# Attention scores on one core: half of the first casts on ScalarE, the first transposes copied by both engines, and an even spread of transposing steps

## The chip, the cores and the metric

The kernel runs on one core of a Trainium2 chip. The metric is the device time of one execution in microseconds (us), the median of several runs. A profile's span is about 1.8 us shorter than the timed run it belongs to (200.7 against 202.5), because it starts and ends with recorded instructions. Some executions are slower, at a lower granted TensorE clock; they are called slow here (in one kernel below 170.88 us at a clock of 0.77, where its fast ones took 164.4 to 166.6 at 0.93 to 0.97).

Engine names in the profile: PE is TensorE's matmuls, PEld its weight loads, DVE is VectorE, ACT is ScalarE, POOL is GpSimd, SP is SyncE, whose queue issues the transfers. HBM is the chip's main memory, SBUF the core's working memory, and PSUM the memory into which the matmuls write. The DMA engines move the bytes of a transfer, in packets; the DMA queue is the list of transfers that they are given. To evacuate is to copy a result out of PSUM.

## The reference

For q and k of shape (8, 8, 512, 64) in float32 the kernel computes all scaled products:

```python
scale = 1.0 / np.sqrt(q.shape[-1])
return (np.einsum('bhqd,bhkd->bhqk', q, k) * scale).astype(np.float32)
```

The inputs are 16.78 MB and the output is 67.11 MB. Nothing can be left out of either, so 83.89 MB have to pass between HBM and SBUF.

## The kernel before

The work is cut into four units (two batches each) and each unit into four store tiles of 4.19 MB. A unit's keys and queries are loaded (2.10 MB each), cast to bfloat16, transposed on PE through PSUM (tile `tp`), and copied into `kT` and `qz`. Score matmuls then fill PSUM tiles `ps`, and ACT and DVE in turn scale them into an SBUF tile `big`, which is stored. Load tiles and store tiles share the three buffers of `big`.

```python
big_pool = ctx.enter_context(tc.tile_pool(name="big", bufs=3))
tpsum_pool = ctx.enter_context(tc.tile_pool(name="tpsum", bufs=2, space=bass.MemoryType.PSUM))
psum_pool = ctx.enter_context(tc.tile_pool(name="psum", bufs=2, space=bass.MemoryType.PSUM))
# ... (cut)
def load_and_cast(v):
    xf = big_pool.tile([P, 2, 2, J * D], f32, name="big")
    both = []
    for x, src in enumerate((k_r, q_r)):
        nc.sync.dma_start(out=xf[:, x], in_=src[v].rearrange("p (s c) -> p s c", s=2))
    for x in range(2):
        xb = bf_pool.tile([P, JP, 2, D, 2], bf16, name="xb")
        wide = (1, RO)[x]
        for s in range(2):
            pinned(nc.gpsimd.tensor_copy(
                out=xb[:, :, s].rearrange("p (g i) d e -> p g e i d", i=wide),
                in_=xf[:, x, s].rearrange("p (g e i d) -> p g e i d", e=2, i=wide, d=D)))
        # ... (cut)

def rearrange(tp, pattern, dst):
    nonlocal n_tp
    copy = (nc.vector.tensor_copy, nc.scalar.copy)[n_tp % 2]
    n_tp += 1
    for s in range(2):
        src = tp[half(s)].rearrange(pattern, n=N, h=2)
        for h in range(2):
            pinned(copy(out=dst(s, h), in_=src[:, h]))
            yield
# ... (cut)
cast = [load_and_cast(v) for v in range(UNITS)]
ts = {}
for _ in transpose(0, *cast[0]):
    pass
for v in range(UNITS):
    ahead = transpose(v + 1, *cast[v + 1]) if v + 1 < UNITS else iter(())
    for t in range(TILES):
        for n, _ in enumerate(scores(v, t)):
            take(ahead, 1 if v == 0 else int(n in (0, 2, 3, 5, 6)))
```

`transpose` is a generator of 20 steps (four transpose tiles, each one step of matmuls and four copies). `take` weaves these steps of the next unit between the eight evacuations of a store tile. The casts write every second bfloat16 element, so that a pair of sequence positions forms one 4-byte word for the transposes.

Of the kernel before, what the change touches and what calls it, by code (L numbers as in the profile page):

```python
# [1 line left out]

# [5 lines left out]


@with_exitstack  # L10
def kernel(
    ctx: ExitStack,
    tc: tile.TileContext,
    q: bass.AP,
    k: bass.AP,
    out: bass.AP,
):







    nc = tc.nc
    B, H, S, D = q.shape
    scale = 1.0 / (D ** 0.5)
    P = 128
    UNITS = B // 2
    N = H  # L30
    M = P // (2 * H)
    R = S // M
    J = R // 2
    RO = 8
    U = S // RO
    JP = J // 2
    JJ = J // RO // 2
    W = 8
    IW = W // JJ
    TILES = N // 2  # L40

    f32 = mybir.dt.float32
    bf16 = mybir.dt.bfloat16

    q_r = q.rearrange("(v b) g (m j) d -> v (b g m) (j d)", b=2, j=R)
    k_r = k.rearrange("(v b) g (m j) d -> v (b g m) (j d)", b=2, j=R)
    out_r = out.rearrange("(v b) (t x h) (u i) k -> v (b t) (h u) x (i k)", b=2, x=2, h=2, i=RO)

    consts = ctx.enter_context(tc.tile_pool(name="consts", bufs=1))

    big_pool = ctx.enter_context(tc.tile_pool(name="big", bufs=3))
    bf_pool = ctx.enter_context(tc.tile_pool(name="bf", bufs=6))
    t_pool = ctx.enter_context(tc.tile_pool(name="t", bufs=2))
    tpsum_pool = ctx.enter_context(tc.tile_pool(name="tpsum", bufs=2, space=bass.MemoryType.PSUM))
    psum_pool = ctx.enter_context(tc.tile_pool(name="psum", bufs=2, space=bass.MemoryType.PSUM))


    pinned = tc.keep_in_program_order

    n_evac = 0  # L60
    n_tp = 0

    def evacuate(dst, src):
        nonlocal n_evac
        if n_evac % 2 == 0:
            pinned(nc.scalar.mul(out=dst, in_=src, mul=scale))  # L66
        else:
            pinned(nc.vector.tensor_scalar(out=dst, in0=src, scalar1=scale, scalar2=None,  # L68
                                           op0=mybir.AluOpType.mult))
        n_evac += 1  # L70

    def half(h):
        return slice(h * D, (h + 1) * D)

    def words(ap):
        return ap.bitcast(f32)

    def load_and_cast(v):

        xf = big_pool.tile([P, 2, 2, J * D], f32, name="big")  # L80
        both = []
        for x, src in enumerate((k_r, q_r)):
            nc.sync.dma_start(out=xf[:, x], in_=src[v].rearrange("p (s c) -> p s c", s=2))
        for x in range(2):
            xb = bf_pool.tile([P, JP, 2, D, 2], bf16, name="xb")

            wide = (1, RO)[x]
            for s in range(2):
                pinned(nc.gpsimd.tensor_copy(  # L89
                    out=xb[:, :, s].rearrange("p (g i) d e -> p g e i d", i=wide),  # L90
                    in_=xf[:, x, s].rearrange("p (g e i d) -> p g e i d", e=2, i=wide, d=D)))
            both.append(words(xb.rearrange("p j s d e -> p j (s d e)")))
        return both

    def rearrange(tp, pattern, dst):

        nonlocal n_tp
        copy = (nc.vector.tensor_copy, nc.scalar.copy)[n_tp % 2]
        n_tp += 1
        for s in range(2):  # L100
            src = tp[half(s)].rearrange(pattern, n=N, h=2)
            for h in range(2):
                pinned(copy(out=dst(s, h), in_=src[:, h]))  # L103
                yield

    def transpose(v, kb, qb):


        kT = t_pool.tile([P, N, M, 2, J], bf16, name="kT")
        qz = qzs[v % 2]  # L110
        ts[v] = (kT, qz)
        kw = words(kT)
        qw = words(qz)
        for j0 in range(0, JP, W):
            tp = tpsum_pool.tile([P, W, P], f32, name="tp")
            for j in range(W):
                pinned(nc.tensor.transpose(out=tp[:, j, :], identity=identity, in_=kb[:, j0 + j]))  # L117
            yield
            yield from rearrange(tp, "d j (n h m) -> d h n m j",
                                 lambda s, h: kw[half(h), :, :, s, j0:j0 + W])  # L120
        for i0 in range(0, RO, IW):
            tp = tpsum_pool.tile([P, IW, JJ, P], f32, name="tp")
            for i in range(IW):
                for jj in range(JJ):
                    pinned(nc.tensor.transpose(out=tp[:, i, jj, :], identity=identity,  # L125
                                               in_=qb[:, RO * jj + i0 + i]))
            yield
            yield from rearrange(tp, "d i jj (n h m) -> d h i n m jj",
                                 lambda s, h: qw[half(h), i0:i0 + IW, :, h * U // 2:(h + 1) * U // 2]
                                 .rearrange("d i n (m s jj) -> d s i n m jj", s=2, jj=JJ)[:, s])  # L130

    def scores(v, t):

        kT, qz = ts[v]
        o = big_pool.tile([P, 2, RO, S], f32, name="big")
        for x in range(2):
            n = 2 * t + x
            for i in range(0, RO, 2):
                ps = psum_pool.tile([P, 2, S], f32, name="ps")
                for w in range(2):  # L140
                    pinned(nc.tensor.matmul(out=ps[:, w, :], lhsT=qz[:, i + w, n, :],  # L141
                                            rhs=kT[:, n].rearrange("d m s j -> d (m s j)"),
                                            start=True, stop=True))
                evacuate(o[:, x, i:i + 2, :], ps)
                yield
        nc.sync.dma_start(out=out_r[v, t], in_=o.rearrange("p x i k -> p x (i k)"))  # L146

    def take(steps, count):
        for _ in range(count):
            next(steps, None)  # L150

    identity = consts.tile([P, P], dtype=f32)
    make_identity(nc, identity)
    qzs = [consts.tile([P, RO, N, P], bf16, name=f"qz{n}") for n in range(2)]
    for qz in qzs:
        nc.vector.memset(qz, 0.0)  # L156
    cast = [load_and_cast(v) for v in range(UNITS)]

    ts = {}
    for _ in transpose(0, *cast[0]):  # L160
        pass
    for v in range(UNITS):
        ahead = transpose(v + 1, *cast[v + 1]) if v + 1 < UNITS else iter(())
        for t in range(TILES):
            for n, _ in enumerate(scores(v, t)):

                take(ahead, 1 if v == 0 else int(n in (0, 2, 3, 5, 6)))
        for _ in ahead:
            pass


# [1 line left out]
_INS = ['q', 'k']  # L173
_OUTS = [((8, 8, 512, 512), 'float32')]


# [23 lines left out]
```

## Time and profile before

| | before |
|---|---|
| time, median of 3 | 202.47 us (202.41 to 202.62) |
| DMA packets' share of 16 engines' span | 98.3% |
| DVE, PE, ACT, POOL busy | 106.8, 105.3, 85.0, 39.5 us of 200.7 |
| first store issued | 36.81 us |

The table of groups (line, engine, operation, output<-input, shapes, count | busy us, mean ns of one | idle us before it and what ended most of it):

```profile
L89 POOL CAST xb<-big 128x2048 bf16<-128x2048 f32 x16 | 38.8, 2468 | 7.9 <-DMA big<-in_k_dram 7.3
...
L103 ACT COPY kT<-tp 64x512 f32<-64x512 f32 x16 | 9.2, 577 | 15.3 <-PE tp L117 15.1
L103 DVE COPY kT<-tp 64x512 f32<-64x512 f32 x16 | 11.0, 686 | 6.3 <-PE tp L117 6.0
```

The timeline of the first unit's copies on ACT, and then of the same on DVE (start us, us, engine, line, operation, count, idle before it):

```profile
17.15 2.35 ACT L103 COPY kT<-tp 64x512 f32<-64x512 f32 x4 [15.13 <-PE tp L117]
22.21 2.50 ACT L103 COPY qz<-tp 64x512 f32<-64x512 f32 x4 [2.70 <-PE tp L125]
```

```profile
15.45 2.79 DVE L103 COPY kT<-tp 64x512 f32<-64x512 f32 x4 [6.04 <-PE tp L117]
20.71 2.80 DVE L103 COPY qz<-tp 64x512 f32<-64x512 f32 x4 [2.47 <-PE tp L125]
```

Each engine takes a whole transpose tile, four copies in a row, and the two overlap: DVE is at its tile from 15.45 to 18.24, ACT starts on the other at 17.15.

### The profile page before, as it was taken

The numbers are of one execution on the slowest core, as the hardware profiler recorded it, in microseconds if no ns is written. First come the engines' busy times: TensorE is split into PE (matmuls) and PEld (weight loads), VectorE is DVE, ScalarE is ACT, GpSimd is POOL, SyncE is SP. The second block draws the span as 40 slices with busy tenths as digits, with TensorE's granted clock in tenths as the row PEclk, the third lists the DMA queues.
The fourth block names the chain that finished last, engine by engine and source line by source line (L and its number), as shares of the span: only waits on it lengthen the run. The fifth ranks groups of instructions, "written<-read, shape, count | busy, mean of one in ns | idle before, by whom it ended". The sixth has DMA issues, their size and how long they took to land.

```text
span 200.7 us, 1143 instructions
## 1 busy us (share of the span) xinstructions
PE 105.3 (52%) x384; PEld 45.8 (23%) x384; DVE 106.8 (53%) x98; ACT 85.0 (42%) x97; POOL 39.5 (20%) x22
## 2 busy tenths in 40 slices
PE   0035758566657465478637496748585667510000
PEld 0034535223214131224313122312121111100000
DVE  6705538486475976485749357844444444630000
ACT  2004423864755629253844384366435243620000
POOL 1299999995000000000000000000000000000000
PEclk9999576999699999957999759975858858975555
DMA  6999999999999999999999999999999999999994
GB/s 206 424 444 437 421 421 441 434 395 421 434 424 441 428 431 431 433 426 434 431 428 424 434 441 424 431 431 434 424 431 434 431 424 431 428 437 428 428 428 199
DMA packets 5509, 83.95 MB, mean 418 GB/s; under 512 B 384, under 2 KB 384, under 8 KB 384
## 3 DMA queue, kind: packets, MB, share of 16 engines
q1 hardware_dynamic: 5504, 83.89, 98.3%
q8 instruction: 3, 0.05, 0.1%
q14 instruction: 2, 0.02, 0.0%
HBM read 16.78 MB, written 67.11 MB: 418 GB/s over the span
## 4 chain that ended last, share of the span: by engine, by line
DMA 40%; DVE 10%; PE 8%; ACT 6%; issue 1%; ACTq 0%; SPq 0%; DVEq 0%
DMA out_dram<-big 40%; DVE big L68 9%; PE ps L141 8%; ACT big L66 5%; ACT qz L103 1%; DVE qz L103 1%; ACTq L66 0%; SPq L146 0%; DVEq L68 0%
## 5 line engine op out<-in xcount | busy, mean ns | idle before, releaser
L141 PE MATMUL ps<-kT,qz 128*128 128x512 bf16 x256 | 87.6, 447 | 55.5 <-ACT big L66 41.6
L68 DVE TENSOR_SCALAR big<-ps 128x1024 f32<-128x1024 f32 x64 | 78.4, 1224 | 59.8 <-PE ps L141 37.2
L66 ACT ACTIVATE big<-ps 128x1024 f32<-128x1024 f32 x64 | 65.5, 1023 | 73.0 <-PE ps L141 37.2
L141 PEld LDWEIGHTS <-qz 128*128 128x128 bf16 x256 | 27.2, 106 | 111.0 <-issue 97.5
L89 POOL CAST xb<-big 128x2048 bf16<-128x2048 f32 x16 | 38.8, 2468 | 7.9 <-DMA big<-in_k_dram 7.3
L117 PE MATMUL tp<-identity,xb 128*128 128x128 f32 x64 | 11.6, 346 | 13.4 <-POOL xb L89 13.4
L103 ACT COPY kT<-tp 64x512 f32<-64x512 f32 x16 | 9.2, 577 | 15.3 <-PE tp L117 15.1
L103 DVE COPY kT<-tp 64x512 f32<-64x512 f32 x16 | 11.0, 686 | 6.3 <-PE tp L117 6.0
L117 PEld LDWEIGHTS tp<-identity,xb 128*128 128x128 f32 x64 | 10.5, 184 | 15.2 <-POOL xb L89 13.4
L103 DVE COPY qz<-tp 64x512 f32<-64x512 f32 x16 | 11.0, 687 | 2.7 <-PE tp L125 2.5
L103 ACT COPY qz<-tp 64x512 f32<-64x512 f32 x16 | 9.6, 602 | 2.9 <-PE tp L125 2.7
L125 PE MATMUL tp<-identity,xb 128*128 128x128 f32 x64 | 9.4, 300 | 2.5 <-ACT kT L103 2.5
L125 PEld LDWEIGHTS tp<-identity,xb 128*128 128x128 f32 x64 | 8.5, 156 | 4.3 <-issue 3.3
L156 DVE MEMSET qz<- 128x4096 uint32 x2 | 6.9, 3472 | 2.5 <-PEq L184 1.7
L103 ACT ACT_TABLE_LOAD x1 | 1.3, 1283 | 0.7 <-PEq L184 0.7
masks.py:199 POOL TENSOR_SCALAR_AFFINE_SELECT identity<-identity 128x128 f32<-128x128 f32 x1 | 0.3, 292 | 0.1
masks.py:197 POOL MEMSET identity<- 128x128 f32 x1 | 0.2, 204 | 0.3 <-POOLq L184 0.3
L184 POOL MEMSET const-float32-0.0<- 128x1 f32 x1 | 0.1, 98 | 0.2 <-issue 0.2
L184 POOL MEMSET const-bfloat16-1.0<- 128x1 bf16 x1 | 0.1, 101 | 0.0
L184 POOL MEMSET const-uint8-127<- 128x1 uint8 x1 | 0.1, 101 | 0.0
L184 POOL MEMSET const-float32-1.0<- 128x1 f32 x1 | 0.1, 98 | 0.0
## 6 DMA issues: line engine op xcount, KB each, us to landing
out_dram<-big SPq DMA_DIRECT2D x16, 4096.0 KB, 20.7
big<-in_k_dram SPq DMA_DIRECT2D x4, 2048.0 KB, 18.1
big<-in_q_dram SPq DMA_DIRECT2D x4, 2048.0 KB, 22.7
```

Of the source, the lines that this page charges most:

```text
L66: pinned(nc.scalar.mul(out=dst, in_=src, mul=scale))
L68: pinned(nc.vector.tensor_scalar(out=dst, in0=src, scalar1=scale, scalar2=None, op0=mybir.AluOpType.mult))
L89: pinned(nc.gpsimd.tensor_copy(out=xb[:, :, s].rearrange("p (g i) d e -> p g e i d", i=wide), in_=xf[:, x, s].rearrange("p (g e i d) -> p ...
L103: pinned(copy(out=dst(s, h), in_=src[:, h]))
L117: pinned(nc.tensor.transpose(out=tp[:, j, :], identity=identity, in_=kb[:, j0 + j]))
L125: pinned(nc.tensor.transpose(out=tp[:, i, jj, :], identity=identity, in_=qb[:, RO * jj + i0 + i]))
L141: pinned(nc.tensor.matmul(out=ps[:, w, :], lhsT=qz[:, i + w, n, :], rhs=kT[:, n].rearrange("d m s j -> d (m s j)"), start=True, stop=True))
L156: nc.vector.memset(qz, 0.0)
L184: nc = _bacc.Bacc("TRN2", target_bir_lowering=False, num_devices=1)
```

## The change

The intent is to bring the first scores forward: while POOL casts one half of an array, ACT casts the other; both engines share each of the first transposes; and unit 1's transposing is spread over four store tiles instead of two and a half. Loads and casts are separated, so that ACT's casts of unit 1 stand after the first copies in its order.

```diff
-    def load_and_cast(v):
+    def load(v):
         xf = big_pool.tile([P, 2, 2, J * D], f32, name="big")
...
+    def cast(v, xf):
...
-                pinned(nc.gpsimd.tensor_copy(
+                to_bf16 = nc.scalar.copy if s and v < 2 else nc.gpsimd.tensor_copy
+                pinned(to_bf16(
...
-        copy = (nc.vector.tensor_copy, nc.scalar.copy)[n_tp % 2]
+        copies = (nc.vector.tensor_copy, nc.scalar.copy)
+        first = len(ts) == 1
...
-                pinned(copy(out=dst(s, h), in_=src[:, h]))
+                pinned(copies[(n_tp + h * first) % 2](out=dst(s, h), in_=src[:, h]))
...
-    cast = [load_and_cast(v) for v in range(UNITS)]
+    xfs = [load(v) for v in range(3)]
 
     ts = {}
-    for _ in transpose(0, *cast[0]):
+    for _ in transpose(0, *cast(0, xfs[0])):
         pass
+    xfs.append(load(3))
+    casts = [None] + [cast(v, xfs[v]) for v in range(1, UNITS)]
...
-                take(ahead, 1 if v == 0 else int(n in (0, 2, 3, 5, 6)))
+                take(ahead, int(n in (0, 2, 3, 5, 6)))
```

More of the change, by code (lines that the diff above doesn't have):

```diff
@@ L76, in words @@
         return ap.bitcast(f32)
-    def load_and_cast(v):
+    def load(v):
         xf = big_pool.tile([P, 2, 2, J * D], f32, name="big")
-        both = []
         for x, src in enumerate((k_r, q_r)):
             nc.sync.dma_start(out=xf[:, x], in_=src[v].rearrange("p (s c) -> p s c", s=2))
+        return xf
+    def cast(v, xf):
+        both = []
         for x in range(2):
@@ L156 @@
         nc.vector.memset(qz, 0.0)
-    cast = [load_and_cast(v) for v in range(UNITS)]
+    xfs = [load(v) for v in range(3)]
     ts = {}
-    for _ in transpose(0, *cast[0]):
+    for _ in transpose(0, *cast(0, xfs[0])):
         pass
+    xfs.append(load(3))
+    casts = [None] + [cast(v, xfs[v]) for v in range(1, UNITS)]
     for v in range(UNITS):
-        ahead = transpose(v + 1, *cast[v + 1]) if v + 1 < UNITS else iter(())
+        ahead = transpose(v + 1, *casts[v + 1]) if v + 1 < UNITS else iter(())
         for t in range(TILES):
             for n, _ in enumerate(scores(v, t)):
-                take(ahead, 1 if v == 0 else int(n in (0, 2, 3, 5, 6)))
+                take(ahead, int(n in (0, 2, 3, 5, 6)))
         for _ in ahead:
```

## The prediction

> **What bounds the kernel now.** I read the 40 slices first, then the DMA queue, the table of windows, the SyncE queue's own waits, and only then the groups of instructions. In the slices, the DMA row is the mean busy share of the 16 DMA engines and the row below it is what they moved:
>
> ```profile
> DMA  6999999999999999999999999999999999999994
> GB/s 206 424 444 437 421 421 441 434 395 421 434 424 441 428 431 431 433 426 434 431 428 424 434 441 424 431 431 434 424 431 434 431 424 431 428 437 428 428 428 199
> ...
> q1 hardware_dynamic: 5504, 83.89, 98.3%
> ```
>
> Only the first and the last slice are below 9. One queue carries all 83.89 MB (16.78 MB of loads, 67.11 MB of stores) and its packets fill 98.3% of the span of 16 engines. No compute engine is above 53%: DVE 106.8 us and PE 105.3 us of 200.7. The table of windows (columns: stretch, its length, busy us of PE, PEld, DVE, ACT, POOL with counts, clock, DMA share, GB/s) shows where the transfer rate falls short:
>
> ```profile
> 0.00:2.00 2.00, 0.00 (x0) 0.00 (x0) 0.34 (x1) 1.26 (x1) 0.70 (x6) 1.00 0.42 82
> 2.00:4.00 2.00, 0.00 (x0) 0.00 (x0) 2.00 (x1) 0.02 (x1) 0.00 (x0) 1.00 0.65 221
> ...
> 40.00:42.00 2.00, 1.52 (x9) 0.71 (x8) 1.03 (x1) 1.30 (x3) 2.00 (x2) 1.00 0.93 328
> 42.00:60.00 18.00, 11.03 (x40) 4.28 (x40) 12.29 (x13) 10.60 (x13) 5.78 (x3) 0.91 1.01 432
> 60.00:196.00 136.00, 75.25 (x262) 28.90 (x261) 72.23 (x67) 59.91 (x66) 0.00 (x0) 0.79 1.01 430
> 196.00:200.70 4.70, 0.00 (x0) 0.00 (x0) 0.00 (x0) 0.00 (x0) 0.00 (x0) 0.50 0.43 185
> ```
>
> Between 4 and 196 us the rate is 430 GB/s, except for one dip at 40 to 42, where the queue passes from loads to stores. At 430 GB/s throughout, 83.95 MB would take 195.2 us, so 5.5 us of the span are lost. The first 4 us moved 0.61 MB, worth 1.4 us, so they lost 2.6; the dip lost 2 x (430 - 328)/430 = 0.5; the last 4.7 us moved 0.87 MB, worth 2.0, so they lost 2.7. That is 5.8, which covers the 5.5. The SyncE queue's waits (engine, line, whom it waited for: us in total, times, longest) say the same from the other side:
>
> ```profile
> SPq L146 <- DVE big L68: 152.5, 16, 17.6
> ```
>
> The sixteen store issues sit in wait for the last evacuation of their tile for 152.5 us, and still the DMA engines are full: earlier issues are queued ahead. Compute is late for the issuer and early for the engines. The chain that ended last gives DMA only 40% and mixes in evacuations, because a store tile cannot be refilled until its earlier store has landed; I trust the slices over that share.
>
> **How much spare there is.** By 40.0 us the queue has moved 30 x 393 + 10 x 431 GB/s = 16.1 MB; the last 0.68 MB of loads take 1.6 us, so the first store is needed at about **41.6 us**, and each further one 4.19 MB / 430 GB/s = 9.75 us later. The store issues in the timeline are at 36.81, 47.49, 56.55, 64.24, 72.77 and 80.56; needed at 41.6, 51.4, 61.1, 70.9, 80.6 and 90.4. The spare is 4.8, 3.9, 4.6, 6.6, 7.8 and 9.8 us. The change must eat about **4 us** at one of the first three stores before the engines run dry at all.
>
> **What the Trainium skill says.** "DMA: Bandwidth & Descriptors", section "Where 436 GB/s comes from", puts the ceiling of the 16 ports at 435.2 GB/s, with the ports as the bottleneck. The trace's 430 to 432 is 99% of it. "Perfetto Trace Analysis", section "Roofline", says that one core alone is bounded by its 16 DMA engines at about 435 GB/s and may pass the 358 GB/s share; this run does. "ScalarE: Activation LUTs", section "What ACT_TABLE_LOAD costs", gives 186 ns + 0.833 ns per column for an ACTIVATE with immediates: 1039 ns at 1024 columns, where the trace has 1023. "PSUM — Partial Sum Buffer", section "PSUM bank collisions raise a hardware error", says that two engines on the same bank and the same 32 partitions must be kept apart, ScalarE and VectorE reads included. No copy of the kernel before meets this: each engine takes a transpose tile of its own.
>
> **The change, part by part.** No bytes, matmuls, evacuations or transposes are added or removed; four casts move from POOL to ScalarE, 16 of the copies are dealt out differently, and the steps of unit 1's transposing are spread.
>
> (a) Half the casts of units 0 and 1 on ScalarE. A POOL cast is 2468 ns (x16). On ScalarE I take the slope of its rows, (1023 - 577)/512 = 0.87 ns per column, so 1023 + 1024 x 0.87 = **1.9 us**; the page's formula gives 1.89. Keys of unit 0 are cast at 8.58 + 2.45 = 11.0 instead of 13.44. But the queries of unit 0 land only one 2.1 MB transfer (4.9 us) later, at about 13.4, so both are ready near 15.9, against 18.33, when the fourth load pair could be issued. Gain for the head of the compute: 2.4 us.
>
> (b) Alternating copies of the first unit. In the order of the changed program each of these copies waits for the other engine's copy before it: both read one transpose tile, the collision case of the page. They run **one after another**. Per tile that is 2 x 0.577 + 2 x 0.686 = 2.5 us plus four hand-overs, an estimate of 2.8; four tiles, 11.3 us. Also, ScalarE takes the query cast first (ready 13.4, done 15.4), and the first copy is ScalarE's. So copies run 15.4 to about 26.7. Before they overlapped across tiles and ran 15.45 to 24.7. This part loses about 2 us, instead of halving the time as its form suggests.
>
> (c) ScalarE's casts of unit 1 now stand in its order behind those copies: 26.7 + 2 x 1.9 = 30.5. The first store tile reuses the buffer of unit 1, so its evacuation starts at about 30.6 instead of 28.13 (where DVE and ACT waited for POOL). This eats **2.4 us** of spare.
>
> (d) Five steps a tile instead of eight in unit 0. Before, the tile took 36.81 - 28.13 = 8.7 us, with eight copies beside eight evacuations. Three fewer steps drop three copies (0.6 us each, not all on the path): I take 8 us. First store at 38.6, needed 41.6: **3 us spare**. Second tile: buffer free when POOL has cast unit 2, its data landing at 28 and 33, so 38 as before; start 38.6, 9 us, issue 47.6 (47.49 before), **3.8 spare**. Third: buffer of unit 3, whose queries land at 43; two casts, 48; issue about 57, **4 spare**. Fourth: it now carries five steps where it had none, 8.5 us as later tiles with steps take (72.77 - 64.24); issue 65.5 to 66.5, needed 70.9, **4.4 spare**. From unit 1 on the plan is the old one.
>
> The sum: no store is late, the queue never runs dry, and the time changes by nothing but the dip at 40 to 42 (at most -0.5 us). Prediction **202.4 us**.
>
> **Rivals.** *The queue runs dry at the first stores.* For it: (b) and (c) put ScalarE's share on the path, and 3 us of spare is not much; PE clock drops to 0.5 in places. If the first store came 2 us past 41.6, the time would be 204.5; to be slower by 2% it must be 4 us late, an error of 7 us in my sum. Against it: even serial copies are counted already. *The head start shortens the run.* If the copies did overlap, compute would start 3 to 5 us sooner; the time would still be 202, because loads alone hold the queue to 41.6 and no transfer moves. A gain of 2% (4 us) would need more than all of the dip and most of the loss at both ends, which the change does not touch. *The fourth load pair* goes out 2.4 us sooner, at 15.9, but it is needed only when three units have been moved, near 32: hidden anyway.
>
> **Range and chances.** The three timed runs lie within 0.2 us; the dip can give 0.5; a late store might cost 1. So 201.8 to 203.0. Faster by over 2% has a chance of 0.01, slower 0.02, within 2% the rest.
>
> **What would show it.** In the changed profile: DMA row 9 from the second to the 39th slice, 430 GB/s from 42 to 196; ScalarE casts of 1.9 us (if 3 or more, (a) is off); first copies of DVE and ACT alternating without overlap, done at about 27 (if done by 22, (b) is wrong); first store issued between 36 and 41 and before the loads end. The prediction is wrong if a slice between 8 and 20 falls to 7 or less, meaning a store came late, or if the steady rate itself changes.

## The result, and the profile after

| | before | after |
|---|---|---|
| time, median | 202.48 us (202.41 to 202.62, 4 runs) | 202.81 us (202.49 to 203.11, 4 runs) |
| ratio of fast runs | | 1.0015, 95% interval 0.9997 to 1.0033 |
| ACT, POOL busy | 85.0, 39.5 us | 94.6, 30.0 us |
| first four stores issued | 36.81, 47.49, 56.55, 64.24 us | 38.99, 47.77, 55.44, 64.24 us |

Ratios here are the mean time of one kernel's fast runs over that of the other's of the same rounds, so not quite the ratio of the medians quoted beside them. The time is the same. The slices of the changed kernel, the DMA engines' mean busy share in tenths and the rate under it:

```profile
DMA  6999999999999999999999999999999999999994
GB/s 206 434 428 438 428 431 424 428 434 428 424 434 434 431 424 431 434 428 428 438 428 431 428 438 428 431 421 434 434 431 421 424 428 428 428 431 431 421 431 199
```

Only the first and last slices are below 9, as before. The table of windows (stretch, length, busy us of PE, PEld, DVE, ACT, POOL with counts, clock, DMA share, GB/s):

```profile
40.00:42.00 2.00, 1.08 (x6) 0.39 (x4) 1.91 (x3) 1.02 (x1) 2.00 (x2) 1.00 0.98 418
42.00:60.00 18.00, 10.85 (x51) 5.07 (x51) 13.94 (x14) 11.51 (x13) 5.70 (x3) 1.00 1.01 431
60.00:196.00 136.00, 75.18 (x256) 28.77 (x259) 73.50 (x69) 59.12 (x65) 0.00 (x0) 0.79 1.01 429
```

The dip at 40 to 42 us is smaller (418 GB/s for 328). It was worth less than it looks: the kernel before moved 459 GB/s in the next 2 us, so over 40 to 44 us it lost 0.3 us. And the long stretch runs a little slower, 429.5 GB/s against 430.4 between 60 and 190 us by the packet records of the two traces (start, duration and size of every DMA packet), which is 0.3 us again, so nothing is won. Each of these is one profile. What the change did to the engines is in the groups:

```profile
L94 POOL CAST xb<-big 128x2048 bf16<-128x2048 f32 x12 | 29.3, 2472 | 17.1 <-DMA big<-in_k_dram 12.1
...
L110 DVE COPY kT<-tp 64x512 f32<-64x512 f32 x16 | 11.0, 686 | 8.5 <-ACT kT L110 8.2
L94 ACT CAST xb<-big 128x2048 bf16<-128x2048 f32 x4 | 9.7, 2468 | 8.9 <-DMA big<-in_k_dram 6.5
...
L110 ACT COPY kT<-tp 64x512 f32<-64x512 f32 x16 | 9.2, 576 | 3.2 <-DVE kT L110 3.0
```

Two things are to be seen. ACT's casts take 2468 ns, no less than POOL's. And the last column has changed for the copies: DVE's wait for ACT's and ACT's wait for DVE's. The timeline of ACT, and then of DVE, shows these waits one by one:

```profile
8.51 2.45 ACT L94 CAST xb<-big 128x2048 bf16<-128x2048 f32 x1 [6.50 <-DMA big<-in_k_dram]
13.37 2.47 ACT L94 CAST xb<-big 128x2048 bf16<-128x2048 f32 x1 [2.41 <-DMA big<-in_q_dram]
15.72 0.56 ACT L110 COPY kT<-tp 64x512 f32<-64x512 f32 x1
17.03 0.58 ACT L110 COPY kT<-tp 64x512 f32<-64x512 f32 x1 [0.75 <-DVE kT L110]
...
25.82 0.58 ACT L110 COPY qz<-tp 64x512 f32<-64x512 f32 x1 [0.76 <-DVE qz L110]
26.42 4.82 ACT L94 CAST xb<-big 128x2048 bf16<-128x2048 f32 x2
31.32 1.02 ACT L66 ACTIVATE big<-ps 128x1024 f32<-128x1024 f32 x1
```

```profile
16.31 0.68 DVE L110 COPY kT<-tp 64x512 f32<-64x512 f32 x1 [6.91 <-ACT kT L110]
17.65 1.41 DVE L110 COPY kT<-tp 64x512 f32<-64x512 f32 x2 [0.65 <-ACT kT L110]
```

ACT copies from 15.72 to 16.28, DVE from 16.31 to 16.99, ACT from 17.03: one after another (DVE's pair at 17.65 is the last copy of one tile and the first of the next). They end at 26.4, where they ended at 24.7 before. ACT's casts of unit 1 follow, and the first evacuation starts at 31.32 instead of 28.13.

### The profile page after: what moved, and what is told of

Its sections match the earlier page's. It is cut to its first block, busy times and chain, and to the rows that moved or that the text cites. A ratio compares the mean times of both kernels' runs of the same rounds, so it can differ in the third digit from the quotient of the medians.

```text
span 200.7 us, 1138 instructions
## 1 busy us (share of the span) xinstructions
PE 103.9 (52%) x377; PEld 45.4 (23%) x384; DVE 106.8 (53%) x98; ACT 94.6 (47%) x101; POOL 30.0 (15%) x18
## 4 chain that ended last, share of the span: by engine, by line
DMA 41%; ACT 10%; DVE 10%; PE 8%; POOL 2%; issue 2%; POOLq 1%; ACTq 0%; SPq 0%; DVEq 0%
DMA out_dram<-big 41%; DVE big L68 8%; ACT big L66 8%; PE ps L148 7%; POOL xb L94 2%; POOLq L204 1%; ACT xb L94 1%; ACT qz L110 1%; DVE qz L110 1%; DVE kT L110 1%; ACT kT L110 1%; PE tp L132 0%; ACTq L66 0%; SPq L153 0%; DVEq L68 0%
## 5 line engine op out<-in xcount | busy, mean ns | idle before, releaser
L148 PE MATMUL ps<-kT,qz 128*128 128x512 bf16 x249 | 85.5, 447 | 54.1 <-ACT big L66 34.6
L66 ACT ACTIVATE big<-ps 128x1024 f32<-128x1024 f32 x64 | 65.5, 1023 | 67.3 <-PE ps L148 34.2
L94 POOL CAST xb<-big 128x2048 bf16<-128x2048 f32 x12 | 29.3, 2472 | 17.1 <-DMA big<-in_k_dram 12.1
L94 ACT CAST xb<-big 128x2048 bf16<-128x2048 f32 x4 | 9.7, 2468 | 8.9 <-DMA big<-in_k_dram 6.5
```

Of the source, the lines that this page charges most:

```text
L66: pinned(nc.scalar.mul(out=dst, in_=src, mul=scale))
L94: pinned(to_bf16(out=xb[:, :, s].rearrange("p (g i) d e -> p g e i d", i=wide), in_=xf[:, x, s].rearrange("p (g e i d) -> p g e i d", e=2, ...
L148: pinned(nc.tensor.matmul(out=ps[:, w, :], lhsT=qz[:, i + w, n, :], rhs=kT[:, n].rearrange("d m s j -> d (m s j)"), start=True, stop=True))
```

## The experiments

My theory: the transfer queue sets the time, is never empty in either kernel, and the change only uses up part of the spare before the first stores. Rival 1: compute is on the path, and gains and losses of the change cancel. Rival 2: the change does shorten the compute, and the queue hides it. Twelve kernels were run; each ran beside the kernel before on its chip.

### The changed kernel again

No edit.

> The changed kernel unedited, timed again in five rounds to settle whether the four first runs (202.49 to 203.11) differ from the kernel before. Theory (the DMA queue sets the time and is never empty): 202.4 to 202.9, ratio within 0.998 and 1.003. Rival (the changed order of compute costs a real few tenths): ratio above 1.002 with an interval clear of 1.

Measured: 202.63 us (202.38 to 202.79, 5 runs) against 202.56 (202.40 to 203.01, 9 runs), ratio 1.0000, interval 0.9987 to 1.0012. The 0.3 us of the first four runs did not come back.

### Part (b) undone

```diff
-                pinned(copies[(n_tp + h * first) % 2](out=dst(s, h), in_=src[:, h]))
+                pinned(copies[(n_tp + 1) % 2](out=dst(s, h), in_=src[:, h]))
```

> The changed kernel with part (b) undone: each engine again copies a whole transpose tile of the first unit. Theory: first copies overlap, the last ends near 22.5 us instead of 26.4, first store issued near 35 us instead of 39.0, and the time stays within 0.3% of the kernel before, because the queue has no room for it before 41.6 us. Rival (the compute head is on the path): 3 to 4 us faster, 199.

Measured: 202.49 us (202.46 to 202.52), ratio 0.9996 (0.998 to 1.0011). With a tile of its own for each engine, the query copies overlap again (DVE, then ACT):

```profile
20.18 2.80 DVE L110 COPY qz<-tp 64x512 f32<-64x512 f32 x4 [4.30 <-PE tp L132]
21.89 2.46 ACT L110 COPY qz<-tp 64x512 f32<-64x512 f32 x4 [3.78 <-PE tp L132]
```

The copies end at 24.35 and the first store is issued at 37.79, not at 35. So undoing the alternation brings the first store forward by 1.2 us, less than the 4 I expected. The copies ended 2.0 us sooner instead of 3.9, since with ACT's query cast in front the overlap was shorter than I drew it. And the edit does a second thing: it swaps the engines of all later transpose tiles back to those of the kernel before, so that the copies beside the first store tile are DVE's again, and that tile took 8.5 us (from 29.26) instead of 7.7. The time does not follow.

### Part (a) undone

```diff
-                to_bf16 = nc.scalar.copy if s and v < 2 else nc.gpsimd.tensor_copy
+                to_bf16 = nc.gpsimd.tensor_copy
```

> The changed kernel with part (a) undone: all casts on POOL, in the new program order. Theory: keys ready at 13.4 us, alternating copies from about 15.4 to 26, unit 1 cast by POOL at 28.1, first store issued near 36 us, earlier than with the ScalarE casts, and the time within 0.3% of before. Rival (the ScalarE casts are what helps the head): first store later than 39 us.

Measured: 202.66 us (202.54 to 202.83), ratio 1.0005 (0.9991 to 1.0019). The first store is issued at 36.14. Moving casts to ACT therefore makes the first store 2.9 us later (38.99), although it makes the first bfloat16 keys ready about 2.3 us sooner (near 11.0 instead of 13.25): ACT's casts of unit 1 then stand behind its copies, while POOL alone had unit 1 done at 28 us.

### Part (d) undone

```diff
-                take(ahead, int(n in (0, 2, 3, 5, 6)))
+                take(ahead, 1 if v == 0 else int(n in (0, 2, 3, 5, 6)))
```

> The changed kernel with part (d) undone: one transposing step after every pair of score matmuls in unit 0, as before. Theory: evacuation starts at 31.3 us, eight copies beside eight evacuations, first store issued near 40 us, second near 48.5, needed at 41.6 and 51.4: still in time, the same 202.5 us. Rival: the first store is late and the time rises by 1 us or more.

Measured: 202.57 us (202.49 to 202.74), ratio 1.0001 (0.9988 to 1.0015). First stores at 39.16, 47.68 and 57.66: the spread of steps moves the first by 0.2 us only, the third by 2.2.

### More casts on ACT, in two doses

These make the first store late on purpose, to find where the spare ends. The first edit gives ACT both halves of unit 1, the second also both halves of unit 0.

```diff
-                to_bf16 = nc.scalar.copy if s and v < 2 else nc.gpsimd.tensor_copy
+                to_bf16 = nc.scalar.copy if v == 1 or (s and v == 0) else nc.gpsimd.tensor_copy
```

> The changed kernel with both halves of unit 1 cast by ScalarE (two more casts of 2.45 us there, 4.9 us). Theory: evacuation starts near 36.2 us, first store issued near 43.9, that is 2.3 us after the 41.6 at which the loads end; the queue stands empty for 2.3 us and never gets them back: 204.8 us, +1.1%. Rival 1 (compute sets the time): +4.9 us, 207.4. Rival 2 (all of it is hidden): 202.5.

```diff
-                to_bf16 = nc.scalar.copy if s and v < 2 else nc.gpsimd.tensor_copy
+                to_bf16 = nc.scalar.copy if v < 2 else nc.gpsimd.tensor_copy
```

> The changed kernel with all casts of units 0 and 1 on ScalarE, four more than in the change. Theory: queries of unit 0 cast at 18.3, copies to 29.0, casts of unit 1 to 38.8, first store issued near 46.6, 5.0 us after 41.6: 207.5 us, +2.5%. Rival 1 (compute sets the time): 2.4 + 4.9 = 7.3 us more, 209.8. Rival 2 (hidden): 202.5.

Measured: 206.88 us (206.67 to 207.63), ratio 1.0229 (1.0209 to 1.0249), first store issued at 43.85; and 209.59 us (209.24 to 209.92), ratio 1.0350 (1.0334 to 1.0365), first store issued at 46.48. The issue times were within 0.2 us of what I wrote; the times were 2.1 us above it in both. The windows of the first dose (columns as above) show the empty queue:

```profile
41.00:42.00 1.00, 0.68 (x3) 0.28 (x3) 0.86 (x1) 0.93 (x2) 1.00 (x1) 1.00 0.58 246
42.00:43.00 1.00, 0.77 (x4) 0.25 (x4) 0.46 (x1) 0.97 (x2) 0.95 (x2) 1.00 0.00 0
43.00:44.00 1.00, 1.00 (x10) 0.93 (x9) 0.77 (x1) 0.88 (x2) 1.00 (x1) 1.00 0.00 0
44.00:44.50 0.50, 0.50 (x5) 0.23 (x4) 0.00 (x0) 0.43 (x1) 0.50 (x1) 1.00 0.00 0
44.50:45.00 0.50, 0.50 (x3) 0.18 (x2) 0.28 (x1) 0.00 (x0) 0.50 (x1) 1.00 1.23 524
```

The last load packets start by about 41.6 (246 of 430 GB/s in that microsecond), as predicted. By the packet records of the trace the last of them ends at 42.12, and the store's first packet starts at 44.77, 0.92 us after its issue at 43.85. In the second dose these are 42.19 and 47.40, again 0.92 us after the issue at 46.48. I had left this delay out. From 40 to 60 us the two doses moved 361 and 305 GB/s; at 430 GB/s the same bytes would take 3.2 and 5.8 us less. About 0.2 of each is the lower rate after the hole, so the holes are worth about 3.0 and 5.6 us. Counted back from the two issues, the real deadline for issuing the first store is near **40.9** (an estimate from these figures), not 41.6. The rest of the loss, 1.4 and 1.5 us, lies later: between 60 and 190 us these two runs moved 427 and 426 GB/s, where the kernel before moved 430. Over the 150 us that remain this is 1.0 and 1.4 us. Why the rate stays lower after a hole is not settled.

Rival 1 expected 207.4 and 209.8. By the totals alone it did better than my theory, 0.5 and 0.2 us off against 2.1. What tells them apart is the shape. From the change to the first dose the first store moved by 4.9 us and the median by 4.3; but from the kernel with all casts on POOL to the changed one it moved by 2.9 us (36.14 to 38.99), and the time did not move (202.66 and 202.63). There is a threshold between 39.2 and 43.8, and the hole in the windows is what stands there.

### One store cut in half

```diff
-        nc.sync.dma_start(out=out_r[v, t], in_=o.rearrange("p x i k -> p x (i k)"))
+        if (v, t) == (2, 0):
+            nc.sync.dma_start(out=out_r[v, t][:, :1], in_=o[:, :1].rearrange("p x i k -> p x (i k)"))
+        else:
+            nc.sync.dma_start(out=out_r[v, t], in_=o.rearrange("p x i k -> p x (i k)"))
```

> The changed kernel with one store in the middle (first tile of unit 2) cut to its first half, a wrong result on purpose; all compute is kept. Theory (the queue is the bound throughout): 2.10 MB less at 430 GB/s, 4.9 us less, 197.6 us, -2.4%. Rival (compute or buffers set the pace in the middle): less than 1 us.

Measured: 197.71 us (197.47 to 198.00), ratio 0.9764 (0.9749 to 0.9779), 4.8 us less for 2.10 MB less in the middle of the run with all compute kept. This is what decides against rival 1: as long as the queue is never empty, the bytes set the time.

### All stores cut in half, before and after

In both kernels the store issues only its first half (wrong results), so that compute sets the time.

```diff
-        nc.sync.dma_start(out=out_r[v, t], in_=o.rearrange("p x i k -> p x (i k)"))
+        nc.sync.dma_start(out=out_r[v, t][:, :1], in_=o[:, :1].rearrange("p x i k -> p x (i k)"))
```

> The kernel before with every store cut to its first half, a wrong result on purpose; all compute is kept. The queue then carries 50.3 MB, 117 us of work at 430 GB/s, and compute sets the time. First tiles as before (third tile starts at 48 when unit 3 is cast), then 8.5 us a tile: about 170 us. Rival (the stores are latency bound, not by bytes): 200.

> The changed kernel with every store cut to its first half, to see what the change does to the compute alone. Theory: both kernels wait until 48 us for the casts of unit 3, and the changed one still has transposing steps in the tile after that, so it is 0 to 2 us slower than the kernel before so cut, about 171. Rival (the change shortens the compute and the queue hid that): 3 us or more faster.

Measured: before so cut, three fast runs of 164.41, 165.74 and 166.59 us (and one slow one of 170.88); after so cut, three of 164.38, 165.34 and 166.05 (one slow, 169.96). The means are 165.6 and 165.3. They are 4.4 and 5.7 us faster than I estimated, and they do not differ by more than their scatter. With the queue no longer the bound, the change buys nothing measurable. (The DMA share falls to between 1 and 3 tenths in every other slice of the first, whose profile is of the slow run, and to between 4 and 7 in most later slices of the second.) Rival 2, at 3 us or more, falls. The scatter of 2 us would hide a gain or loss of about 1 us.

### What an ACT cast costs

After the last evacuation, while the last stores drain, ACT runs these forms twice on a tile of ones. The result stays right.

```diff
+    for rep in range(2):
+        pinned(nc.scalar.copy(out=y1, in_=x))
+        pinned(nc.scalar.copy(out=y2[:, :, 0], in_=x))
+        pinned(nc.scalar.copy(out=y3, in_=x))
+        pinned(nc.scalar.copy(out=y1[:, :512], in_=x[:, :512]))
+        pinned(nc.scalar.mul(out=y1, in_=x, mul=scale))
+        pinned(nc.scalar.mul(out=y2[:, :, 0], in_=x, mul=scale))
```

> The changed kernel with ScalarE probes after the last evacuation, while the last stores drain, result right: copies of 128x1024 float32 in SBUF to dense bfloat16, to bfloat16 at every second element, to dense float32, of 128x512 to dense bfloat16, and the scaled form (the evacuation's operation) on the first two. The change's casts took 1.20 ns a column where I had estimated 0.93. If the stride costs it: 1.23 us for the strided form and about 1.0 for the dense. If SBUF as source costs it: 1.23 us for all of the copies of 1024. If the copy operation costs it: 1.23 for the copies and 1.02 for the scaled forms.

Measured: one look, 202.59 us. The groups of ACT by shape:

```profile
L188 ACT CAST bf_stride<-probe_in 128x1024 bf16<-128x1024 f32 x2 | 2.6, 1324 | 0.0
L192 ACT ACTIVATE bf_stride<-probe_in 128x1024 bf16<-128x1024 f32 x2 | 2.6, 1320 | 0.0
L191 ACT ACTIVATE bf_dense<-probe_in 128x1024 bf16<-128x1024 f32 x2 | 2.1, 1056 | 0.1
L189 ACT COPY f_dense<-probe_in 128x1024 f32<-128x1024 f32 x2 | 2.1, 1033 | 0.0
L187 ACT CAST bf_dense<-probe_in 128x1024 bf16<-128x1024 f32 x2 | 2.1, 1026 | 0.0
...
L190 ACT CAST bf_dense<-probe_in 128x512 bf16<-128x512 f32 x2 | 1.2, 614 | 0.0
```

Writing every second bfloat16 element costs 1.32 us against 1.03 dense, whichever operation does it; SBUF as source or the copy operation cost nothing extra. The cast's 2468 ns at 2048 columns against 1324 at 1024 gives 1.12 ns a column for the strided form; the dense one has (1026 - 614)/512 = 0.80. A dense cast of 2048 would take about 1.85 us by that slope (an estimate), which is what I had put down for the strided one.

### Two tries for the head

The only time left outside the steady rate is at both ends. Two kernels tried to start the engines sooner with a second queue.

```diff
-            nc.sync.dma_start(out=xf[:, x], in_=src[v].rearrange("p (s c) -> p s c", s=2))
+            (nc.sync, nc.scalar if v == 0 else nc.sync)[x].dma_start(out=xf[:, x], in_=src[v].rearrange("p (s c) -> p s c", s=2))
```

> The changed kernel with the queries of unit 0 loaded by ScalarE's DMA queue, so that two queues start at once. The first 4 us of the span lose 2.6 us of transfer time. If the issue of 0.4 us each on one queue is what holds the start, this saves up to 0.5 us: 202.0. If the first packets' own latency holds it, nothing: 202.5. Keys and queries of unit 0 would then land together at about 13.4, which delays the keys' cast by 4.9 us and the first store to perhaps 40 to 41.

Measured: 204.44 us (203.89 to 204.85), ratio 1.0088 (1.0064 to 1.0111). The first slice moved 236 GB/s instead of 206, about 0.35 us gained. But keys and queries then land together at 13.2 us, the first evacuation starts at 33.5 and the first store is issued at 42.03, later than 40.9, and a slice falls to 320 GB/s. By the packet records no packet is under way from 42.05 to 42.95, and between 60 and 190 us this run moves 427 GB/s, like the two doses. So the threshold lies between 39.2 and 42.0.

The second kernel also has part (b) undone, and splits the first keys by partitions, half on each queue:

```diff
+            if v == 0 and x == 0:
+                nc.sync.dma_start(out=xf[:D, x], in_=s_r[:D])
+                nc.scalar.dma_start(out=xf[D:, x], in_=s_r[D:])
+            else:
+                nc.sync.dma_start(out=xf[:, x], in_=s_r)
```

> The version with the most spare that the runs point to: the changed kernel with part (b) undone, and the first keys loaded by two queues, each half of the partitions, so that the engines fill sooner but no data lands later. Theory: the loads by two queues gained about 0.3 us in the first slice (236 GB/s for 206) before they lost it to a late store; here nothing is late, so 202.2 us, at most 0.4 us under the kernel before. Rival (64 partitions in one transfer do not fill the 16 engines): keys land later than 8.5 us and the time is 202.5 to 203.

Measured: 207.46 us (207.26 to 207.97), ratio 1.0251 (1.0237 to 1.0265), far beyond what either side expected. Its windows:

```profile
4.00:8.00 4.00, 0.00 (x0) 0.00 (x0) 3.20 (x2) 0.00 (x0) 0.00 (x0) 1.00 0.95 201
8.00:12.00 4.00, 0.00 (x0) 0.00 (x0) 1.41 (x1) 1.28 (x1) 0.00 (x0) 1.00 1.00 250
12.00:16.00 4.00, 0.00 (x0) 0.00 (x0) 0.00 (x0) 1.10 (x1) 1.07 (x1) 1.00 0.97 336
16.00:40.00 24.00, 13.51 (x59) 8.70 (x60) 11.43 (x15) 17.40 (x16) 16.11 (x8) 0.86 1.01 429
```

The busy share is full, but at half the rate; in the packet records, packets of 16 KB took 1.28 us (the median) between 4 and 8 us instead of 0.61. The keys landed at 14.9 us instead of 8.5. Against 430 GB/s the three windows lose 2.1, 1.7 and 0.9 us, 4.7 of the 4.9 in all. I should have looked this up: the Trainium skill, "SBUF — State Buffer", section "Door 1: The DMA port swizzle", says that partitions 0 to 63 reach only 8 of the 16 ports and 64 to 127 the other 8, at 27.2 GB/s a port, so 218 GB/s for either half. The run's 201 and 250 are near what one half alone may move, although both were in flight. Why the two halves did not add up, no run here tests. No version beat the kernel before.

## Why the prediction was right, point by point

**The bound.** Shown. No slice but the first and last is below 9 after the change, and taking 2.10 MB away took 4.8 us away (4.9 expected).

**(a) The casts.** The step was mis-sized: 2.47 us for 1.9, because I took the slope from dense writes. Keys and queries were ready near 15.9 all the same, because the queries land at 13.4 and are cast in another 2.47 on either engine. Further down it cost 0.5 us for each of ACT's casts, or 1.0 us for unit 1's two (4.82 for 3.8). The copies before them ended 0.3 us sooner than predicted, so the evacuation came at 31.3 instead of 30.6.

**(b) The copies.** Shown: alternating, without overlap, done at 26.4 against 26.7 predicted and 24.7 before. That they follow one another comes from the waits in the program and shows in the timeline, and with part (b) undone the copies of two engines overlap again. The shared output is not the reason: in the kernel before, both engines wrote `kT` at once, from 17.15 to 18.24. That leaves the shared PSUM tile. The collision that the prediction takes from the page explains only part of this. A tile's four copies read partitions 0 to 63 twice and then 64 to 127 twice, so the second hand-over of the three is between different partitions, which is not the page's case; yet ACT, at 17.03, waited there for DVE too. The wait is thus wider than that rule asks for. That the program guards the tile as a whole would fit, but no run here tests it.

**(c) The order on ACT.** Shown by undoing (a): 36.14 against 38.99.

**(d) The spread of steps.** For the first store 0.2 us by the run that undoes it; the tile took 7.7 us from 31.3, as against the 8 that I took.

**The spare.** The first store came at 38.99 (38.6 predicted). The deadline was near 40.9, not 41.6, since a store's first packet starts 0.92 us after the issue. So 1.9 us were left where I had 3. The verdict stood, with less room than I said. What a late store costs was mis-sized as well: the prediction counts it one for one (2 us past 41.6 gives 204.5, and 2% takes 4 us, an error of 7 us in its sum). Measured, an issue 2.3 us past 41.6 cost 4.4 us, and moving the first store by 4.9 us (38.99 to 43.85) was enough for 2.3%. This did not come into play, but the margin behind the chance of 0.02 was smaller than stated.

**The later tiles.** The second store was issued at 47.77 (47.6 predicted), the third at 55.44 (57), the fourth at 64.24 (65.5 to 66.5). The third and fourth were better than I feared.

**The rivals.** The empty queue is real, but lies beyond the change: it takes a first store past 40.9. The chance of 0.01 for a gain rested on the queue never waiting, and it did not wait. The head start did not exist (the first store came 2.2 us later than before), and where the first store did come sooner (36.14 with all casts on POOL) the time stayed, as the prediction said it would.

## What to carry to other kernels

First ask when each transfer must be issued, and compare that deadline with when it is issued; work that ends before the deadline can move by microseconds, in either direction, and the time stays. Sharing one PSUM tile between two engines put them in single file here; with a tile each they overlapped. Handing work to a second engine in the same program order can delay what stands behind it on that engine more than it helps what is in front.

## What the Trainium skill lacked or had wrong

- "ScalarE: Activation LUTs", "What ACT_TABLE_LOAD costs": its 186 ns and 0.833 ns a column fit dense output here (1039 ns at 1024 columns, 1026 measured), but it has nothing on strided writes: 1324 ns at 1024 and 2468 at 2048 columns for every second bfloat16 element, 1.12 ns a column.
- "SBUF — State Buffer", "Door 1: The DMA port swizzle": its note on 16-byte lines says that bfloat16 can be strided by up to 8 elements for free. ScalarE's writes at a stride of 2 took 1.32 us where dense ones took 1.03.
- No page has it: after the queue had stood empty, for 0.9 us (two queues) to 5.2 us (the second dose) by the packet records, the rate between 60 and 190 us stayed at 426 to 427 GB/s in all three such runs, against 430 in the kernel before. The cause is open.
